# First projection by turns: keys and values over pairs of feature chunks, with the loads in that order on two queues

## The chip, the cores and the metric

One core of one Trainium2 chip runs the kernel, 1 core in all. The metric is the device time of one execution in microseconds (us). The kernel before has 923.12 us, the median of 3 runs (920.76 to 924.27).

## The reference, cut to what matters

The reference is a long chain of layers on 256 tokens of width 1024. The change touches the beginning of the first layer:

```python
h = rms_norm(x, norm_pre)                  # x: 256 tokens x 1024 features, float32
proj = h @ w_in                            # 1024 x 6936
(q_n, k_c, v_c, k_s, v_s, k_w, v_w, g_n, z_n,
 q_r, k_r, v_r, z_r, m_a, m_b) = jnp.split(proj, split_points(), axis=-1)
k_c, k_s, k_w, q_n = (rotated by position)
o_a = nsa(q_n, k_c, v_c, k_s, v_s, k_w, v_w, g_n)      # attention
o_b = retention(q_r, k_r, v_r)
x = x + rms_norm(merged @ w_out, norm_post)
```

A second layer (state space, latent attention, cross attention) and a mixture of 32 experts follow.

## The kernel before, in words

**Precision.** A product of two float32 matrices is made from three passes of a faster type: each operand is split into a high half (a rounded copy) and a low half (the rest), and `mm3` (L235 to L240) adds high by high (L238), high by low (L239) and low by high (L240). For a weight, `piece` (L219) issues the load on SP's queue (L226), ScalarE copies the high half (L231), and VectorE subtracts it to get the low half (L232). A feature chunk of x is 128 features by 256 tokens. `turn(c)` (L618) makes its two halves, on ScalarE (L619) and on VectorE (L620), and multiplies by the gain of the norm on the way.

**The first projection.** The 1024 features are eight chunks of 128. A weight piece covers a pair of chunks and one group of output columns. So a group takes four pieces. The first group, called K here, has 512 columns (three key parts and one value part, array `w1`, pieces 0 to 3). The second, V, has 280 columns (two value parts and the gates, array `w1b`, pieces 0 to 3). The third, Q, is `w1` pieces 4 to 7. K0 to K3, V0 to V3 and Q0 to Q3 are these pieces below. `tokmaj` (L242) is a generator that does one piece per step: 12 matmuls for 2 blocks of tokens, 2 chunks and 3 passes; the last step also evacuates the two PSUM banks of the group.

**Normalization.** The sum of squares per token comes from `x0`, the copy of x that is laid out by token. ScalarE squares and adds it in `scales()` (L499), GpSimd takes the power (L507), and VectorE scales the tables of cosines (L510). The results are scaled on evacuation, so the matmuls don't wait for it. `row()` (L512) turns the factors into a row with two small products on TensorE (L520).

**Order.** `early()` (L594) gives the order K0 to K3, V0 to V3, Q0 to Q3, then the rest. In the starting stage the instructions are pinned to the order of the code; afterwards a scheduler orders each engine. `self.first` holds pieces that were loaded ahead. The script of attention (L1010) weaves its steps with steps of the projection: a number means so many pieces. `keys` transposes the rotated keys (L338), `build`, `h0` to `h3` (L843) and `gelu` compress them, `queries` and `rows` are the attention itself.

**Queues.** SP's queue carries the weights and the big constants, ScalarE's queue (ACTq) the first loads of x by feature (`xT`, three loads: chunks 0 to 1, 2 to 3, 4 to 7) and the gain (`gpre`). Eight semaphores serve all loads in turn, so that the ninth load is not issued before the first has landed. The weights lie in a pool of five buffers (`w4`); a load into a used buffer waits for the low half that was made from it. Seven matmuls on a constant (`warm`, L1978) occupy TensorE until the first operands are there.

```python
w0 = self.sb("w4", [P, 2, 512])
for k in range(2):
    pin(nc.sync.dma_start(out=w0[:, k], in_=t["w1"][0][:, 512 * k:512 * k + 512]))
for c in (slice(0, 2), slice(2, 4), slice(4, 8)):
    pin(nc.scalar.dma_start(out=xT[:, c].rearrange("p k n -> p (k n)"), in_=t["xT"][:, 256 * c.start:256 * c.stop]))
```

The end of the program is the mixture of experts, whose weights (1 MB a load) come through 24 buffers.

Of the kernel before, what the change touches and what calls it, by code (L numbers as in the profile page):

```python
# [21 lines left out]
P = 128  # L22
# [79 lines left out]
def cols(v):  # L102

    return v.reshape(-1, P).T


def prepare(inp):

    a = {}
    f = {k: np.asarray(v) for k, v in inp.items()}  # L110
    g = {k[:-2]: (v[0] if v.shape[0] == 1 else v) for k, v in f.items() if k.endswith("_2")}
    a["x"] = f["x"].reshape(2, P, 1024).transpose(1, 0, 2).reshape(P, 2048)
    a["xT"] = f["x"].reshape(256, 8, P).transpose(2, 1, 0).reshape(P, 2048)
    a["gpre"] = cols(f["norm_pre"])
    a["mem"] = g["mem"].reshape(2, P, 1024).transpose(1, 0, 2).reshape(P, 2048)
    a["pos"] = g["positions"].reshape(2, P).T

# [43 lines left out]
    c = constants()  # L161
# [22 lines left out]
class K:  # L184
# [31 lines left out]
        v = self.tiles[which][:, o:o + math.prod(shape[1:])]  # L216
        return v.rearrange("p (a b) -> p a b", b=shape[-1]) if len(shape) == 3 else v.rearrange("p (a b c) -> p a b c", b=shape[-2], c=shape[-1])

    def piece(self, name, i, kc, n):  # L219

        if (name, i) in self.first:
            return self.first.pop((name, i))
        nc = self.nc
        pin = self.tc.keep_in_program_order if self.starting else lambda ins: ins
        s = self.sb("w4", [P, kc, n])
        nc.sync.dma_start(out=s.rearrange("p k n -> p (k n)"), in_=self.t[name][i])  # L226
        h = self.sb("hl", [P, 2, kc, n], F32R)
# [14 lines left out]
    def tokmaj(self, name, i0, np_, kc, n, x, evac, tag="pa"):  # L242

        ps = [self.ps(tag, [P, 512])[:, :n] for _ in range(2)]
# [225 lines left out]
    def block1(self):  # L470
        nc = self.nc
        pin, t = self.tc.keep_in_program_order, self.t


        gain = self.sb("st", [P, 8])
        xT = self.sb("a8", [P, 8, 256])


        w0 = self.sb("w4", [P, 2, 512])
        for k in range(2):  # L480
            pin(nc.sync.dma_start(out=w0[:, k], in_=t["w1"][0][:, 512 * k:512 * k + 512]))
        for c in (slice(0, 2), slice(2, 4), slice(4, 8)):
            pin(nc.scalar.dma_start(out=xT[:, c].rearrange("p k n -> p (k n)"), in_=t["xT"][:, 256 * c.start:256 * c.stop]))
            if c.start == 0:
                pin(nc.scalar.dma_start(out=gain, in_=t["gpre"]))
# [13 lines left out]
        def scales():  # L499

            ss = self.sb("sm", [P, 2])
            junk = self.sb("a8", [P, 2, 1024])
            for t in range(2):
                self.sumsq(self.x0[:, t], ss[:, t:t + 1], junk[:, t])
# [87 lines left out]
            return ev  # L592

        def early():  # L594
            yield from self.tokmaj("w1", 0, 4, 2, 512, h, ev_k)
            yield from self.tokmaj("w1b", 0, 4, 2, 280, h, ev_v)
            yield from self.tokmaj("w1", 4, 4, 2, 512, h, ev_q)
            yield from self.featmaj("w1", 8, 4, 2, h, ev_zn)
            for i in range(2):
                yield from self.tokmaj("w1", 12 + 4 * i, 4, 2, 512, h, ev_r(i))  # L600
            for nt in range(2):
                yield from self.tokmaj("w1", 20 + 4 * nt, 4, 2, 512, h, ev_vr(nt))
# [8 lines left out]
                yield from self.tokmaj("w1", 28 + 4 * nt, 4, 2, 512, h, ev_zr(nt))  # L611

        main = chain(early(), late())
        self.warm(7, idle)
        hl = self.sb("hl", [P, 2, 2, 512], F32R)
        self.first["w1", 0] = self.chunks(hl)(0), self.chunks(hl)(1)

        def turn(c):  # L618
            pin(nc.scalar.activation(hh[:, 0, c], xT[:, c], AF.Copy, scale=gain[:, c:c + 1]))  # L619
            pin(nc.vector.scalar_tensor_tensor(hh[:, 1, c], xT[:, c], gain[:, c:c + 1], hh[:, 0, c].bitcast(F32), OP.mult, OP.subtract))  # L620

        for k in range(2):
            pin(nc.scalar.activation(hl[:, 0, k], w0[:, k], AF.Copy))
            pin(nc.vector.tensor_tensor(hl[:, 1, k], w0[:, k], hl[:, 0, k].bitcast(F32), OP.subtract))
            turn(k)
        next(main)
        for i in range(1, 4):
            self.first["w1", i] = self.piece("w1", i, 2, 512)
            if i == 2:
                for j in range(2):  # L630
                    pin(nc.sync.dma_start(out=self.x0[:, j], in_=t["x"][:, j * 1024:(j + 1) * 1024]))
            turn(2 * i)
            turn(2 * i + 1)
            if i == 3:
                pin(nc.sync.dma_start(out=self.tiles["cst"], in_=t["cst"]))
                pin(nc.sync.dma_start(out=self.tiles["row"], in_=t["row"][0].partition_broadcast(P)))
                pin(nc.sync.dma_start(out=self.tiles["vec"], in_=t["vec"]))
                pin(nc.sync.dma_start(out=self.ident, in_=t["ident"]))
                scales()
            next(main)  # L640
        row()
        self.starting = False
        script, oT = self.nsa(kcv, qn, vsw, gate)
# [251 lines left out]
    def nsa(self, kcv, qn, vsw, gate):  # L895
# [73 lines left out]
        def rows(hh, g, t):  # L969
            def f():  # L970
                if t == 0:
                    s["pt", hh, g] = self.sb("a4", [P, 2, 384])
                qT, ksw, pt = s["qT"], s["ksw"], s["pt", hh, g]
                h = 4 * g + hh
                n = (t + 1) * P
                ps = self.ps("pb", [P, 2, n])
                for i in range(2):
                    nc.tensor.matmul(ps, qT[g][:, hh, t * P:(t + 1) * P], ksw[i][:, g, :, 0:n], start=(i == 0), stop=(i == 1))
                p = self.softmax(ps, 2, n, scale, cm[:, 256 - n:256], gate[:, t, 3 * h + 1:3 * h + 3])
                s["p", hh, g, t] = p  # L980
            return f
# [25 lines left out]

        flow = [(hh, g, t) for hh in range(4) for g in range(2) for t in range(2)]
        build, h0, h1, h2, h3, gelu, project = self.compress(s)
        script = [3, keys, 1, build, 2, h0, 1, h1, 1, h2, 1, h3, 1, gelu, 1, queries, rows(*flow[0]), 1, project]  # L1010
        for i, (hh, g, t) in enumerate(flow):
            if i > 0:
                script += [rows(hh, g, t), 1]
# [1126 lines left out]
```

## Time and profile before

| | |
|---|---|
| median of 3 runs | 923.12 us (920.76 to 924.27) |
| the profiled execution: its own time | 920.25 us |
| its span in the profile | 918.5 us |
| TensorE busy | 888.0 us (97%) |
| VectorE busy | 567.1 us (62%) |
| ScalarE busy | 456.9 us (50%) |
| moved by DMA | 232.17 MB, mean 253 GB/s |
| mean granted TensorE clock | 0.994 |

The profile shows one execution. Its own time is 1.75 us longer than its span, and lies 2.87 us below the median of the runs. A matmul's record ends when its last result is out, so that records overlap; how fast TensorE goes is seen from the distance between starts.

### The profile page before, as it was taken

Reading aid. Unit: us, or ns where it says so; the run is one execution under the profiler, and the core shown is the slowest. Engines: PE = TensorE matmul, PEld = TensorE weight load, DVE = VectorE, ACT = ScalarE, POOL = GpSimd, SP = SyncE. Lnnn points to the kernel's source line nnn. Section 1 sums busy time; section 2 is a strip of 40 time slices with the busy share of each in tenths; the row PEclk is TensorE's granted clock in tenths of the full one; section 3 lists DMA queues with packets and bytes.
Section 4 is the critical chain, followed back from the end, with each engine's and each line's share of the span. In section 5 each row is a group of like instructions: output and inputs, shape, how many; then the busy total and the mean of one; then the engine's idle time right before and its main releaser. Section 6 shows DMA issues by size and latency. Waiting matters only on the chain.

```text
span 918.5 us, 14740 instructions
## 1 busy us (share of the span) xinstructions
PE 888.0 (97%) x5633; PEld 697.7 (76%) x5633; DVE 567.1 (62%) x1222; ACT 456.9 (50%) x837; POOL 23.8 (3%) x43
## 2 busy tenths in 40 slices
PE   9999999999999999999999999999999999996885
PEld 6788888878899999988999897888998644442422
DVE  5689865676675999977799868556454521110103
ACT  6655666454465778777758565336453211111012
POOL 0000000100010000000000000000000000000001
PEclk9999999999999999999999999999999999999998
DMA  8945454555656554545556555668978999999994
GB/s 307 388 139 184 161 173 159 185 176 175 234 190 201 183 175 128 172 162 177 176 199 235 175 188 192 221 237 296 401 285 333 378 420 421 420 419 421 420 421 188
DMA packets 50553, 232.17 MB, mean 253 GB/s; under 512 B 6000, under 2 KB 6192, under 8 KB 37808
## 3 DMA queue, kind: packets, MB, share of 16 engines
q1 hardware_dynamic: 49760, 230.15, 68.2%
q8 instruction: 45, 0.74, 0.3%
q10 hardware_dynamic: 720, 1.05, 0.3%
q14 instruction: 28, 0.23, 0.1%
HBM read 226.95 MB, written 4.23 MB: 252 GB/s over the span
## 4 chain that ended last, share of the span: by engine, by line
PE 79%; DMA 18%; DVE 1%; ACT 1%; issue 0%; SPq 0%; POOL 0%; DVEq 0%; ACTq 0%
PE pa L238 19%; PE pa L239 19%; PE pa L240 19%; DMA wc<-in_wgu_dram 6%; DMA wf<-in_wdn_dram 4%; DMA wa<-in_wgu_dram 4%; DMA wf<-in_wdl_dram 2%; PE pb L239 2%; PE pb L240 2%; PE pb L238 2%; PE pb L1420 1%; PE pb L338 1%; PE pb L1321 1%; PE pb L2061 1%; PE pb L2024 1%; DMA w<-in_w_dram 1%
## 5 line engine op out<-in xcount | busy, mean ns | idle before, releaser
L232 DVE TENSOR_TENSOR hl<-w,hl 128x1024 fp32r<-128x1024 f32 (+3 forms) x214 | 252.1, 1186 | 112.7 <-ACT hl L231 112.2
L231 ACT ACTIVATE hl<-w 128x1024 fp32r<-128x1024 f32 (+3 forms) x214 | 218.4, 1030 | 178.3 <-PE pa L240 127.9
L238 PE MATMUL pa<-hl,a 128*128 128x512 f32 (+3 forms) x398 | 155.8, 393 | 0.3 <-ACT a L619 0.2
L239 PE MATMUL pa<-hl,a 128*128 128x512 f32 (+3 forms) x398 | 152.5, 384 | 0.4 <-DVE hl L232 0.4
L240 PE MATMUL pa<-hl,a 128*128 128x512 f32 (+3 forms) x398 | 152.3, 384 | 0.0
L238 PE MATMUL pa<-a,hl 128*128 128x256 f32 x456 | 133.3, 292 | 0.0
L239 PE MATMUL pa<-a,hl 128*128 128x256 f32 x456 | 128.7, 282 | 0.0
L240 PE MATMUL pa<-a,hl 128*128 128x256 f32 x456 | 128.6, 282 | 0.0
L238 PEld LDWEIGHTS pa<-a,hl 128*128 128x128 f32 x456 | 86.9, 191 | 1.7 <-issue 0.9
L239 PEld LDWEIGHTS pa<-a,hl 128*128 128x128 f32 x456 | 87.0, 191 | 0.4
L240 PEld LDWEIGHTS pa<-a,hl 128*128 128x128 f32 x456 | 86.9, 191 | 0.0
L238 PEld LDWEIGHTS pa<-hl,a 128*128 128x128 f32 x398 | 74.6, 188 | 15.6 <-ACT a L619 1.3
L240 PEld LDWEIGHTS pa<-hl,a 128*128 128x128 f32 x398 | 74.7, 188 | 15.1 <-DVE a L620 0.4
L239 PEld LDWEIGHTS pa<-hl,a 128*128 128x128 f32 x398 | 74.8, 188 | 14.9 <-DVE hl L232 1.7
L2067 ACT ACTIVATE vec<-pb,sm 128x256 f32<-128x256 f32 x8 | 3.8, 475 | 96.9 <-PE pb L2061 89.9
L238 PE MATMUL pa<-hl,b 128*128 128x512 f32 x128 | 51.3, 400 | 0.0
L239 PE MATMUL pa<-hl,b 128*128 128x512 f32 x128 | 50.1, 391 | 0.0
L240 PE MATMUL pa<-hl,b 128*128 128x512 f32 x128 | 50.1, 391 | 0.0
L2047 DVE TENSOR_SCALAR sm<-pb 128x1 f32<-128x1 f32 x8 | 1.3, 158 | 61.2 <-PE pb L2043 61.2
L2068 DVE SCALAR_TENSOR_TENSOR vec<-vec,pb 128x256 f32<-128x256 f32 x8 | 3.4, 421 | 53.1 <-ACT vec L2067 53.1
L397 ACT ACTIVATE a<-a,st 128x128 f32<-128x128 f32 (+1 forms) x64 | 28.5, 446 | 13.5 <-DVE st L394 13.3
L2098 PE MATMUL pa<-wz 128*128 128x512 f32 (+1 forms) x64 | 31.7, 619 | 0.1
(418 smaller groups left out, 1410.8 us busy)
## 6 DMA issues: line engine op xcount, KB each, us to landing
w<-in_w_dram SPq DMA_DIRECT2D x107, 512.0 KB, 4.1
wa<-in_wgu_dram SPq DMA_DIRECT2D x28, 1024.0 KB, 18.4
w<-in_wxkv_dram SPq DMA_DIRECT2D x16, 512.0 KB, 4.4
w<-in_wso_dram SPq DMA_DIRECT2D x16, 512.0 KB, 4.2
wa<-in_wdn_dram SPq DMA_DIRECT2D x8, 1024.0 KB, 17.5
wb<-in_wdn_dram SPq DMA_DIRECT2D x8, 1024.0 KB, 18.6
wc<-in_wgu_dram SPq DMA_DIRECT2D x8, 1024.0 KB, 19.2
wd<-in_wgu_dram SPq DMA_DIRECT2D x8, 1024.0 KB, 19.8
```

Of the source, the lines that this page charges most:

```text
L231: pin(nc.scalar.activation(hi, src, AF.Copy))
L232: pin(nc.vector.tensor_tensor(lo, src, hi.bitcast(F32), OP.subtract))
L238: mm(ps, l[0], r[0], start=first, stop=False)
L239: mm(ps, l[0], r[1], start=False, stop=False)
L240: mm(ps, l[1], r[0], start=False, stop=last)
L338: self.nc.tensor.transpose(ps[:, b, t * P:(t + 1) * P], src[t][:, c * P:(c + 1) * P], self.ident)
L397: nc.scalar.activation(p[:, i], s[:, i], AF.Exp, bias=st[:, 0, i:i + 1], scale=-1.0, accum_out=st[:, 1, i:i + 1])
L1321: nc.tensor.matmul(ps[:, b], s["q", hf][:, hh, t * P:(t + 1) * P], s["k", hf][:, hh, 0:n], start=True, stop=True)
L1420: nc.tensor.matmul(po[64 * q:64 * q + 64, b, sl], x[:, hh * 64:hh * 64 + 64], m[:, hh], start=(i < 2), stop=(i != 1))
L2024: pin(nc.tensor.matmul(g[c][:, b], self.x0[:, t, (c + b) * P:(c + b + 1) * P], s["s32"][:, t], start=(t == 0 and b == 0), stop=(t == 1 and ...
L2061: self.pinned(self.nc.tensor.matmul(s["pg"][32 * e:32 * e + 32], s["xg"][:, k, 32 * e:32 * e + 32], s["up"][k][:, e], start=(k == 0), stop ...
L2098: self.pinned(self.nc.tensor.matmul(acc[t][h][:, o:o + n], s["sT"][:, t * P:(t + 1) * P], y, start=(q == 0), stop=(q == 7)))
```

## The change

K and V go by turns: K0, V0, K1, V1, K2, V2, V3, K3. Each has its own two PSUM banks, taken ahead. The loads are issued in the order of use, on two queues: ScalarE's carries chunks 0 to 1 of x with the gain in front of them, V0, chunks 2 to 3, V1; SP's carries K0, K1, chunks 4 to 5, K2, V2, then x by token, chunks 6 to 7, V3, the constants, K3. The separate load of the gain is gone. x by feature lies in another pool (`b16`). Two pieces of Q come before `row()`, `keys` is the first step of the script, and two pieces fewer stand in the script before `h0`. There are 6 warming matmuls in place of 7.

```diff
-    a["xT"] = f["x"].reshape(256, 8, P).transpose(2, 1, 0).reshape(P, 2048)
-    a["gpre"] = cols(f["norm_pre"])
+    a["xT"] = np.concatenate([cols(f["norm_pre"]), f["x"].reshape(256, 8, P).transpose(2, 1, 0).reshape(P, 2048)], axis=1)
...
+        room = self.sb("b16", [P, 2056])
+        gain, xT = room[:, 0:8], room[:, 8:].rearrange("p (k n) -> p k n", k=8)
+        def features(c, queue=nc.scalar):
+            a = 0 if c == 0 else 8 + 256 * c
+            pin(queue.dma_start(out=room[:, a:8 + 256 * c + 512], in_=t["xT"][:, a:8 + 256 * c + 512]))
...
+        features(0)
+        pin(nc.scalar.dma_start(out=wv[0].rearrange("p k n -> p (k n)"), in_=t["w1b"][0]))
+        features(2)
+        pin(nc.scalar.dma_start(out=wv[1].rearrange("p k n -> p (k n)"), in_=t["w1b"][1]))
...
         def early():
-            yield from self.tokmaj("w1", 0, 4, 2, 512, h, ev_k)
-            yield from self.tokmaj("w1b", 0, 4, 2, 280, h, ev_v)
...
-        self.warm(7, idle)
+        self.warm(6, idle)
...
-        next(main)
-        for i in range(1, 4):
-            self.first["w1", i] = self.piece("w1", i, 2, 512)
-            if i == 2:
+        banks = [[self.ps("pa", [P, 512]) for _ in range(2)] for _ in range(2)]
+        keys = self.tokmaj("w1", 0, 4, 2, 512, h, ev_k, ps=banks[1])
+        values = self.tokmaj("w1b", 0, 4, 2, 280, h, ev_v, ps=banks[0])
+        next(keys)
+        for i in range(1, 8):
+            if i in (1, 3):
+                self.first["w1b", i // 2] = self.piece("w1b", i // 2, 2, 280, wv[i // 2])
+            elif i == 2:
+                self.first["w1", 1] = self.piece("w1", 1, 2, 512)
+                turn(2)
+                turn(3)
+                features(4, nc.sync)
+            elif i == 4:
+                self.first["w1", 2] = self.piece("w1", 2, 2, 512)
+                turn(4)
+                turn(5)
+            elif i == 5:
+                self.first["w1b", 2] = self.piece("w1b", 2, 2, 280)
                 for j in range(2):
                     pin(nc.sync.dma_start(out=self.x0[:, j], in_=t["x"][:, j * 1024:(j + 1) * 1024]))
+            elif i == 6:
+                features(6, nc.sync)
+                self.first["w1b", 3] = self.piece("w1b", 3, 2, 280)
+                turn(6)
+                turn(7)
                 pin(nc.sync.dma_start(out=self.tiles["cst"], in_=t["cst"]))
+                self.first["w1", 3] = self.piece("w1", 3, 2, 512)
...
+                scales()
+            next(keys if i in (2, 4, 7) else values)
+            if i == 6:
+                self.first["w1", 4] = self.piece("w1", 4, 2, 512)
...
+        next(main)
+        next(main)
         row()
...
-        script = [3, keys, 1, build, 2, h0, 1, h1, 1, h2, 1, h3, 1, gelu, 1, queries, rows(*flow[0]), 1, project]
+        script = [keys, 1, build, 1, h0, 1, h1, 1, h2, 1, h3, 1, gelu, 1, queries, rows(*flow[0]), 1, project]
```

SP's queue at its start, before (`w` are weights, `x` is x by token):

```order
L481 DMA w_3_105<-in_w_dram 128x512 x2
L226 DMA w_21_158<-in_w_dram 128x1024
L226 DMA w_23_179<-in_w_dram 128x1024
L631 DMA x_58<-in_x_dram 128x1024 x2
L226 DMA w_25_202<-in_w_dram 128x1024
L635 DMA cst<-in_cst_dram 128x1208
L636 DMA row<-in_row_dram 128x124
L637 DMA vec<-in_vec_dram 128x773
L638 DMA ident<-in_ident_dram 128x128
L226 DMA w_40_272<-in_w1b_dram 128x560
```

SP's queue at its start with the change (`b_1_103` holds x by feature):

```order
L486 DMA w_2_104<-in_w_dram 128x512 x2
L227 DMA w_24_174<-in_w_dram 128x1024
L482 DMA b_1_103<-in_xT_dram 128x512
L227 DMA w_27_211<-in_w_dram 128x1024
L227 DMA w_29_232<-in_w1b_dram 128x560
L648 DMA x_58<-in_x_dram 128x1024 x2
L482 DMA b_1_103<-in_xT_dram 128x512
L227 DMA w_31_252<-in_w1b_dram 128x560
L654 DMA cst<-in_cst_dram 128x1208
L227 DMA w_33_262<-in_w_dram 128x1024
```

K3 (`w_25_202` before, `w_33_262` now) moves from behind x by token to behind the constants.

ScalarE after K0, before (L231 is the high half of a weight, L619 of a chunk, L331 the sum of squares, L528 an evacuation of K):

```order
L231 ACTIVATE hl_160<-w_21_158 128x1024
L619 ACTIVATE a_5_115<-a_2_104,st_103 128x256 x2
L231 ACTIVATE hl_181<-w_23_179 128x1024
L619 ACTIVATE a_5_115<-a_2_104,st_103 128x256 x2
L331 ACTIVATE a_28_216,sm_215<-x_58 128x1024
L231 ACTIVATE hl_204<-w_25_202 128x1024
L619 ACTIVATE a_5_115<-a_2_104,st_103 128x256 x2
L331 ACTIVATE a_28_216,sm_215<-x_58 128x1024
```

ScalarE after K0 with the change:

```order
L232 ACTIVATE hl_159<-w_3_105 128x560
L232 ACTIVATE hl_176<-w_24_174 128x1024
L621 ACTIVATE a_6_116<-b_1_103 128x256 x2
L232 ACTIVATE hl_196<-w_4_106 128x560
L232 ACTIVATE hl_213<-w_27_211 128x1024
L621 ACTIVATE a_6_116<-b_1_103 128x256 x2
L232 ACTIVATE hl_234<-w_29_232 128x560
L332 ACTIVATE a_36_269,sm_268<-x_58 128x1024
L332 ACTIVATE a_37_271,sm_268<-x_58 128x1024
```

The V pieces (128x560) stand between the K pieces, and both sums of squares come together, ahead of V3, chunks 6 to 7 and K3.

## Rows read from the trace of the kernel before

**Rows 1.** The chain that ended last: start us, us, what.

```profile
6.47 8.01 DMA w<-in_w_dram
15.60 1.24 DVE hl L232
26.36 0.44 PE pb L338 x4
...
746.29 17.12 DMA wc<-in_wgu_dram
883.57 18.62 DMA wf<-in_wdl_dram
```

**Rows 2.** Waits of SP's queue, 540 us to the end: us in total, times, longest.

```profile
SPq L1841 <- PE pb L2061: 16.3, 13, 6.9
```

**Rows 3.** TensorE by time, first 45 us: start us, us, line, count, [idle before].

```profile
1.19 5.56 PE L1984 MATMUL pb<-a 128*128 128x256 f32 x14 [1.19 <-DVE it L1876]
6.94 0.73 PE L238 MATMUL pa<-hl,a 128*128 128x512 f32 x2 [0.19 <-ACT a L619]
...
20.22 0.68 PE L520 MATMUL pb<-a,cst 128*128 128x128 f32 x4 [0.40 <-PE pa L240]
...
22.22 0.29 PE L240 MATMUL pa<-hl,a 128*128 128x280 f32 x1
...
26.07 0.29 PE L240 MATMUL pa<-hl,a 128*128 128x280 f32 x1
...
28.18 0.39 PE L238 MATMUL pa<-hl,a 128*128 128x512 f32 x1
...
30.02 0.39 PE L240 MATMUL pa<-hl,a 128*128 128x512 f32 x1
...
32.97 0.39 PE L238 MATMUL pa<-hl,a 128*128 128x512 f32 x1
...
33.74 1.60 PE L843 MATMUL pb<-a,a 128*32 128x256 f32 x16
...
38.43 1.07 PE L843 MATMUL pb<-a,a 128*32 128x256 f32 x16
```

**Rows 4.** Waits of SP's queue, first 100 us.

```profile
SPq L631 <- DMA a<-in_xT_dram: 3.0, 1, 3.0
```

**Rows 5.** Stretches: us, busy of PE, PEld, DVE, ACT, POOL; clock, DMA share, GB/s.

```profile
5.00:15.00 10.00, 9.81 (x39) 7.11 (x39) 6.30 (x10) 7.42 (x13) 0.00 (x0) 1.00 1.03 410
60.00:70.00 10.00, 10.00 (x52) 8.52 (x52) 9.30 (x40) 6.04 (x16) 0.31 (x1) 1.00 0.01 2
```

**Rows 6.** ScalarE by time, with a load's issue on its queue and one on SP's.

```profile
1.67 0.46 ACTq L483 DMA_DIRECT2D a<-in_xT_dram  x1
1.67 0.42 SPq L226 DMA_DIRECT2D w<-in_w_dram  x1
...
9.20 0.91 ACT L619 ACTIVATE a<-a,st 128x256 fp32r<-128x256 f32 x2
...
12.38 1.04 ACT L331 ACTIVATE a<-x 128x1024 f32<-128x1024 f32 x1
...
19.17 1.22 ACT L231 ACTIVATE hl<-w 128x560 fp32r<-128x560 f32 x2
...
23.31 1.06 ACT L231 ACTIVATE hl<-w 128x1024 fp32r<-128x1024 f32 x1 [0.87 <-PE pa L240]
```

**Rows 7.** VectorE by time.

```profile
9.11 1.23 DVE L232 TENSOR_TENSOR hl<-w,hl 128x1024 fp32r<-128x1024 f32 x1 [0.58 <-ACT hl L231]
...
12.86 0.87 DVE L620 SCALAR_TENSOR_TENSOR a<-a,st,a 128x256 fp32r<-128x256 f32 x2
...
18.58 1.28 DVE L510 TENSOR_SCALAR cst<-cst,st 128x8 f32<-128x8 f32 x8 [0.89 <-POOL st L507]
```

**Rows 8.** Two loads issued at 1.67 us: KB, us to landing.

```profile
w<-in_w_dram SPq DMA_DIRECT2D x1, 512.0 KB, 6.3
...
a<-in_xT_dram ACTq DMA_DIRECT2D x1, 256.0 KB, 7.5
```

More of the change, by code (lines that the diff above doesn't have):

```diff
@@ L217, in spare, with piece @@
         return v.rearrange("p (a b) -> p a b", b=shape[-1]) if len(shape) == 3 else v.rearrange("p (a b c) -> p a b c", b=shape[-2], c=shape[-1])
-    def piece(self, name, i, kc, n):
+    def piece(self, name, i, kc, n, s=None):
         if (name, i) in self.first:
@@ L224, in piece @@
         pin = self.tc.keep_in_program_order if self.starting else lambda ins: ins
-        s = self.sb("w4", [P, kc, n])
-        nc.sync.dma_start(out=s.rearrange("p k n -> p (k n)"), in_=self.t[name][i])
+        if s is None:
+            s = self.sb("w4", [P, kc, n])
+            nc.sync.dma_start(out=s.rearrange("p k n -> p (k n)"), in_=self.t[name][i])
         h = self.sb("hl", [P, 2, kc, n], F32R)
@@ L240, in mm3, with tokmaj @@
         mm(ps, l[1], r[0], start=False, stop=last)
-    def tokmaj(self, name, i0, np_, kc, n, x, evac, tag="pa"):
-        ps = [self.ps(tag, [P, 512])[:, :n] for _ in range(2)]
+    def tokmaj(self, name, i0, np_, kc, n, x, evac, tag="pa", ps=None):
+        ps = [p[:, :n] for p in ps or [self.ps(tag, [P, 512]) for _ in range(2)]]
         for i in range(np_):
@@ L472, in block1 @@
         pin, t = self.tc.keep_in_program_order, self.t
-        gain = self.sb("st", [P, 8])
-        xT = self.sb("a8", [P, 8, 256])
-        w0 = self.sb("w4", [P, 2, 512])
+        room = self.sb("b16", [P, 2056])
[3 more added lines that the diff above has]
+            pin(queue.dma_start(out=room[:, a:8 + 256 * c + 512], in_=t["xT"][:, a:8 + 256 * c + 512]))
+        w0, wv = self.sb("w4", [P, 2, 512]), [self.sb("w4", [P, 2, 280]) for _ in range(2)]
         for k in range(2):
             pin(nc.sync.dma_start(out=w0[:, k], in_=t["w1"][0][:, 512 * k:512 * k + 512]))
[L482 to L485, printed above, removed]
+        features(0)
+        pin(nc.scalar.dma_start(out=wv[0].rearrange("p k n -> p (k n)"), in_=t["w1b"][0]))
+        features(2)
+        pin(nc.scalar.dma_start(out=wv[1].rearrange("p k n -> p (k n)"), in_=t["w1b"][1]))
         pin(nc.scalar.activation(self.mhalf[:, 4:8], self.mhalf[:, 0:4], AF.Tanh))
@@ L501, in scales @@
             ss = self.sb("sm", [P, 2])
-            junk = self.sb("a8", [P, 2, 1024])
             for t in range(2):
-                self.sumsq(self.x0[:, t], ss[:, t:t + 1], junk[:, t])
+                self.sumsq(self.x0[:, t], ss[:, t:t + 1], self.sb("a8", [P, 1024]))
             r = rs["col"] = self.sb("st", [P, 2])
@@ L625, in block1 @@
             turn(k)
-        next(main)
-        for i in range(1, 4):
-            self.first["w1", i] = self.piece("w1", i, 2, 512)
-            if i == 2:
+        banks = [[self.ps("pa", [P, 512]) for _ in range(2)] for _ in range(2)]
[16 more added lines that the diff above has]
+                self.first["w1b", 2] = self.piece("w1b", 2, 2, 280)
                 for j in range(2):
                     pin(nc.sync.dma_start(out=self.x0[:, j], in_=t["x"][:, j * 1024:(j + 1) * 1024]))
-            turn(2 * i)
-            turn(2 * i + 1)
-            if i == 3:
+            elif i == 6:
[3 more added lines that the diff above has]
+                turn(7)
                 pin(nc.sync.dma_start(out=self.tiles["cst"], in_=t["cst"]))
+                self.first["w1", 3] = self.piece("w1", 3, 2, 512)
                 pin(nc.sync.dma_start(out=self.tiles["row"], in_=t["row"][0].partition_broadcast(P)))
+                scales()
+            next(keys if i in (2, 4, 7) else values)
+            if i == 6:
+                self.first["w1", 4] = self.piece("w1", 4, 2, 512)
+                pin(nc.sync.dma_start(out=self.ident, in_=t["ident"]))
+                self.first["w1", 5] = self.piece("w1", 5, 2, 512)
                 pin(nc.sync.dma_start(out=self.tiles["vec"], in_=t["vec"]))
-                pin(nc.sync.dma_start(out=self.ident, in_=t["ident"]))
-                scales()
-            next(main)
+        next(main)
+        next(main)
         row()
```

## The prediction

> **What bounds the kernel now.** I read the views in this order. The chain of waits first, for what sets the end. Its last part is loads of expert weights back to back, from 746.29 us to the one that lands at 902.2 (883.57 + 18.62) [rows 1]. That does not make the beginning worthless: until then SP's queue waits for TensorE to release buffers (16.3 us in 13 waits for L2061 alone) [rows 2]. The stream begins when TensorE has come so far, and its end moves with that. So a microsecond won at the beginning is won at the end, as long as TensorE stays the bound in between.
>
> TensorE by time comes next. In a steady stretch a matmul of 512 columns starts every 0.227 us (13 starts from 30.02 to 32.97), one of 280 columns every 0.128 us (30 starts from 22.22 to 26.07) [rows 3]. K is 48 of the first kind, 10.9 us, V 48 of the second, 6.1 us, together 17.0. But from the first one at 6.94 to the first of Q at 28.18 pass 21.24 us [rows 3]. Between them stand also two small products of `row` and eight transposes, some 12 narrow records at 0.44 us for four [rows 1], 1.3 us. The rest, 21.24 - 17.0 - 1.3 = 2.9 us, is waiting. What it waits for, the chain says: the load issued at 6.47 us that lands at 14.48 is K3, and the low half that ends at 16.84 follows from it (L232) [rows 1]. K3 was issued late, since SP's queue stood 3.0 us for a semaphore that a load of x had [rows 4]. A second wait is at 20.22, where TensorE idles 0.40 us ahead of `row` [rows 3].
>
> **The change part by part.**
>
> *The start.* TensorE's first matmul waited for L619 (0.19 us idle in the record) [rows 3]; L619 had waited for the separate load of the gain. The gain now comes in front of the first chunks. I take the first matmul at 6.6 us instead of 6.94. One warming matmul less takes off 5.56 / 7 = 0.79 us at most [rows 3], ending the warming at 6.0; it lies in the shadow of the first operands and costs nothing. If that cover is gone, because TensorE's clock needed it, the first 12 matmuls would start at twice 0.227 us, at 1.2 in place of 2.4 GHz, and 2.7 us are lost; the clock column reads 1.00 in the stretch from 5 us [rows 5].
>
> *The loads.* They run at 410 GB/s in all [rows 5], which is 400 KB per us. Up to and with K3 the change loads 5824 KB in place of 4100 KB (before, K0 to K2, x by feature, the gain and x by token stood ahead of K3; now V and the constants do too, and the gain rides with x). 1724 KB more are 4.3 us, so K3 lands at 14.5 + 4.3 = 18.8 us. It is needed only after K0 to V3, that is after 6.6 + 36 x 0.227 + 48 x 0.128 = 20.9 us.
>
> How the two queues share decides when the early pieces land. K1 (512 KB on SP's queue) and a load of 256 KB on ScalarE's were issued in the same moment, 1.67 us [rows 6]; the large one landed at 8.0, the small one at 9.2 [rows 8]. So they don't share by bytes, else the small one had been first; rather whole loads take turns. I take turns, and 400 KB per us from 5.6 us on: second half of K0 6.2, V0 6.9, K1 8.2, chunks 2 to 3 8.9, chunks 4 to 5 9.5, V1 10.2, K2 11.5, V2 12.2, x by token 14.8, chunks 6 to 7 15.4, V3 16.1, constants 17.6. With equal bytes K1 would be there at 9.5 and TensorE would lose 0.4 us more in K1.
>
> The Trainium skill, "DMA: Bandwidth & Descriptors", section "Queues, rings and completion order", says that each DMA engine goes round the queues packet by packet; the two landings agree with that, and by it the end of K3 would be the 24.1 us below rather than 24.5. The same page of the Trainium skill, "Issuing engines are not separate DMA queues", speaks against a second queue: it saves issue time alone, no bandwidth. Nothing above counts on bandwidth from it.
>
> *ScalarE and VectorE.* Per K piece ScalarE needs 1.06 + 0.91 us (weight, two chunks), per V piece 0.61 (1.22 / 2), and 1.04 us for each sum of squares [rows 6]; VectorE needs 1.23 + 0.87 for a K piece, some 0.7 for a V piece (scaled from 1.23 by columns), and 1.28 for the tables [rows 7]. In the new order ScalarE handles x by token (landed 14.8) until 16.3, V3 until 17.0, chunks 6 to 7 until 17.9, K3 from 18.9 to 19.9. VectorE first waits for GpSimd's power (0.89 us before) [rows 7] until some 17.5, then V3 18.2, chunks 19.0, tables 20.3, K3 21.5. TensorE reaches V3 at 19.4 and K3 at 20.9. It does the one matmul that needs no low half and waits until 21.5. K3 ends at 21.5 + 11 x 0.227 = 24.0; with 0.1 for the waits in K0, 24.1 us.
>
> *The narrow work.* `row` and the eight transposes still cost 1.3 us, now amid Q, where there are no such waits; I leave 0.3 us for starting them. Equal work is then done at 24.1 + 1.3 + 0.3 = 25.7 us instead of 28.18: -2.5 us.
>
> *After that.* Q0 and Q1 are loaded behind K3, some 1.3 us each and the constants between them, landing by 20.4 and 22; TensorE needs them at 24.1 and 27. No cover is lost. `h0` took 1.60 us before and the same work 1.07 later [rows 3], since the load behind it was late; two more pieces stand ahead of it now, so I take 0.3 of these 0.5 us. Sum: -2.8 us. Attention as a whole stands two pieces (5.5 us) later in TensorE's order and starts 2.5 us earlier by the clock, so its own steps come some 3 us later; the two pieces are missing at the end of the layer, where TensorE has other work in line. At nothing, then, as long as TensorE is the bound there.
>
> **Bounds.** Most: no waiting from 6.6 on, 23.6 for K3, nothing for starting narrow work (23.6 + 1.3 against 28.18), 0.5 at `h0`: -3.8 us. Least: 0, if all of it is waited for elsewhere. I take -2.8, near the upper end, because each load but K3 lands well before its use. The profiled execution would go from 920.25 to 917.45. It lies 2.87 us below the median of the runs, 923.12; against that median I forecast **920.3 us**.
>
> **The rivals.**
>
> *The gain is eaten in attention.* From 60 to 70 us VectorE is busy 9.30 of 10 us [rows 5], close to a bound of its own. If the steps of attention, now later, set the pace there, the 2.8 us are lost again: 923 us. Against it: TensorE is busy 10.00 of 10 there too, with projection pieces between the steps, and has no less work.
>
> *K3 arrives too late, and the kernel is slower.* Its load waits on SP's queue for the buffer of V1 (its low half, some 11.8 us by my times), with everything behind it. A load took 8.01 us from issue to landing [rows 1]. From 11.8 that is 19.8, which costs 1 us. Each microsecond beyond 19 is one on TensorE's path; the gain is used up at about 21.8. If the SP queue stalls twice, at V2's buffer and at this one, for 3.0 us each as before [rows 4], K3 lands at 24 to 25 and ends past 29, later than before by 1 us or more after its narrow work: 924.5 us. For it: V2, V3 and K3 now each wait for a low half on VectorE. Against it: at 12 us there are still 5 us of loads in line.
>
> *It gains more.* The waits of TensorE in attention also shrink because two pieces lie ready more: 2 us more, 918.
>
> *It doesn't do what it says:* the order of the engines shows that the turns are there, so I give this nothing.
>
> **How the numbers follow.** Forecast 0.62; eaten 0.18; slower by late loads 0.10; more 0.10. About 0.5% (4.6 us) is what a measurement of this kernel can tell from no change; the three runs shown lie 3.5 us apart. Faster by over 0.5% means below 918.5: half of "more", a fifth of the forecast by scatter of the medians, 0.17 in all. Slower by over 0.5% means above 927.7: a part of the late loads, 0.06. Within: 0.77. The range reaches down to the largest gain with some scatter, 917.2, and up to the case of late loads, 924.2.
>
> **What would show it.** Right: the chain of waits has no load of K3 in it; the first matmul at 6.6; K and V together take 17 to 18 us with starts at 0.227 and 0.128 us; Q's first matmul at about 24; the stream of expert weights begins some 3 us earlier and goes at the same rate. Wrong: idle TensorE ahead of V3 or K3 (the load, or VectorE behind the tables); first starts at 0.45 us apart (the clock); an equal end of K3 but an unchanged start of the expert stream (attention).

## The result

The change has 926.34 us (median of 13 runs, 924.21 to 928.27); before, in the same comparison, 921.77 us (13 runs). The ratio is 1.0054, 95% interval 1.0043 to 1.0065: slower by 4.6 us, where 920.3 us was forecast. The profiled execution took 926.27 us with a span of 924.5 us (before 918.5).

The start went as forecast or better. TensorE by time (start us, us, engine, line, operation, shape, count, [idle before]):

```profile
5.61 0.73 PE L239 MATMUL pa<-hl,a 128*128 128x512 f32 x2
...
8.51 0.29 PE L239 MATMUL pa<-hl,a 128*128 128x280 f32 x1
...
10.78 0.50 PE L240 MATMUL pa<-hl,a 128*128 128x512 f32 x1 [0.35 <-DVE hl L233]
...
23.86 0.62 PE L239 MATMUL pa<-hl,a 128*128 128x512 f32 x2
```

Against [rows 3] the first matmul is 1.3 us earlier and Q's first 4.3 us (two pieces of Q now precede `row` and the transposes, some 1.3 us of narrow work). The only wait of the engine is the 0.35 us at K1. The load of K3 landed at 18.75 us, and ScalarE took it at once:

```profile
18.86 1.06 ACT L232 ACTIVATE hl<-w 128x1024 fp32r<-128x1024 f32 x1 [1.33 <-DMA w<-in_w_dram]
```

In the chain of waits no load of K3 stands any more, only K1's; the last expert load begins 5.4 us later than in [rows 1]:

```profile
1.67 6.71 DMA w<-in_w_dram
...
888.98 19.19 DMA wf<-in_wdl_dram
```

So the time is lost between. A count over the whole trace shows where: for each matmul the distance to the next start, less the steady distance of its shape (0.227 us for 512 columns, and so on: the lower quartile of the distances behind that shape in the kernel before), added up by stretch. Before loses 12.2 us of TensorE up to 50 us, the change 9.3: 2.9 won. From 50 to 110 us before loses 5.0, the change 9.5; from 170 to 210 us before 2.0, the change 6.9. Elsewhere the two agree within 0.5 us. The stretches (us, busy of PE, PEld, DVE, ACT, POOL, clock, DMA share, GB/s), first before, then the change:

```profile
70.00:80.00 10.00, 10.00 (x51) 8.41 (x50) 9.37 (x26) 5.11 (x11) 0.00 (x0) 1.00 0.90 297
...
190.00:200.00 10.00, 10.00 (x49) 7.96 (x48) 6.76 (x9) 5.23 (x7) 0.00 (x0) 1.00 0.64 193
```

```profile
70.00:80.00 10.00, 7.94 (x27) 5.75 (x26) 9.82 (x25) 1.63 (x3) 0.00 (x0) 0.83 0.43 135
...
190.00:200.00 10.00, 7.57 (x30) 5.90 (x29) 7.17 (x10) 3.33 (x5) 0.56 (x1) 0.83 0.52 156
```

In these two stretches TensorE now idles 2.1 and 2.4 us, and its granted clock falls. **The first loss**, TensorE of the change:

```profile
72.26 0.61 PE L239 MATMUL pa<-hl,a 128*128 128x512 f32 x2
73.57 0.73 PE L239 MATMUL pa<-hl,a 128*128 128x512 f32 x2 [0.69 <-ACT hl L232]
75.67 0.50 PE L240 MATMUL pa<-hl,a 128*128 128x512 f32 x1 [1.37 <-DVE hl L233]
...
76.51 0.63 PE L241 MATMUL pa<-hl,a 128*128 128x512 f32 x1
76.94 0.63 PE L239 MATMUL pa<-hl,a 128*128 128x512 f32 x1
```

It waits for a high and a low half, and then starts matmuls 0.43 us apart, until 79.9 us: 1.2 in place of 2.4 GHz. The low half decides: the high half is there by 73.57 us, the low half only at 75.62. VectorE in that time:

```profile
67.32 1.22 DVE L233 TENSOR_TENSOR hl<-w,hl 128x1024 fp32r<-128x1024 f32 x1
...
68.84 0.40 DVE L381 TENSOR_TENSOR a<-pa,cst 128x256 f32<-128x256 f32 x1
...
73.54 0.42 DVE L386 TENSOR_TENSOR a<-a,a 128x256 f32<-128x256 f32 x1
...
74.41 1.21 DVE L233 TENSOR_TENSOR hl<-w,hl 128x1024 fp32r<-128x1024 f32 x1
```

Between two low halves stand 5.9 us of other work: 12 operations of the rotation (L381 to L386, called ropes below) of retention's first operands, amid a softmax. **The second loss**:

```profile
178.30 1.46 PE L820 MATMUL pb<-a,a 128*128 128x256 f32 x6
...
180.46 0.59 PE L822 MATMUL pb<-a,a 128*128 128x256 f32 x2
...
195.54 0.84 PE L339 MATMUL pb<-ident,a 128*128 128x128 f32 x4 [2.43 <-DVE a L595]
196.03 0.78 PE L241 MATMUL pa<-hl,a 128*128 128x512 f32 x1
196.61 0.63 PE L239 MATMUL pa<-hl,a 128*128 128x512 f32 x1
```

Three steps of retention (the last ones, `outs`, L820 and L822) stand together at 178 to 181 us, each with normalizations on VectorE behind it. These push back what follows there:

```profile
187.87 0.99 DVE L831 TENSOR_SCALAR a<-pb,sm,sm 128x256 f32<-128x256 f32 x2 [0.87 <-POOL sm L327]
...
192.88 1.22 DVE L233 TENSOR_TENSOR hl<-w,hl 128x1024 fp32r<-128x1024 f32 x1
194.02 0.68 DVE L593 SCALAR_TENSOR_TENSOR a<-a,pa 128x512 f32<-128x512 f32 x1
194.74 0.75 DVE L595 SCALAR_TENSOR_TENSOR a<-a,st,a 128x512 f32<-128x512 f32 x1
```

TensorE takes its work in order: the transposes (L339) wait for L595, and the next piece stands behind them.

### The profile page after: what moved, and what is told of

Same layout as the page of the kernel before. It is cut to its first block, busy times and chain, and to the rows that moved or that the text cites. A ratio compares the mean times of both kernels' runs of the same rounds, so it can differ in the third digit from the quotient of the medians.

```text
span 924.5 us, 14745 instructions
## 1 busy us (share of the span) xinstructions
PE 890.0 (96%) x5631; PEld 700.1 (76%) x5631; DVE 567.7 (61%) x1222; ACT 456.0 (49%) x837; POOL 23.8 (3%) x43
## 4 chain that ended last, share of the span: by engine, by line
PE 82%; DMA 11%; DVE 3%; issue 1%; ACT 1%; POOL 0%; SPq 0%; DVEq 0%; ACTq 0%; POOLq 0%
PE pa L239 19%; PE pa L241 19%; PE pa L240 19%; DMA wc<-in_wgu_dram 4%; PE pb L2086 3%; DMA wa<-in_wgu_dram 2%; DMA wf<-in_wdn_dram 2%; DMA wf<-in_wdl_dram 2%; PE pa L2123 2%; PE pb L2049 2%; PE pb L2111 2%; PE pb L240 2%; PE pb L241 2%; PE pb L239 2%; PE pb L1445 1%; PE pb L339 1%
## 5 line engine op out<-in xcount | busy, mean ns | idle before, releaser
L232 ACT ACTIVATE hl<-w 128x1024 fp32r<-128x1024 f32 (+3 forms) x214 | 218.7, 1030 | 183.2 <-PE pa L241 132.8
L239 PE MATMUL pa<-hl,a 128*128 128x512 f32 (+3 forms) x398 | 156.4, 395 | 0.7 <-ACT hl L232 0.7
L239 PE MATMUL pa<-a,hl 128*128 128x256 f32 x456 | 133.4, 293 | 0.0
L239 PEld LDWEIGHTS pa<-a,hl 128*128 128x128 f32 x456 | 86.9, 191 | 2.6 <-issue 1.8
L240 PEld LDWEIGHTS pa<-hl,a 128*128 128x128 f32 x398 | 75.7, 190 | 16.5 <-DVE hl L233 2.7
L239 PEld LDWEIGHTS pa<-hl,a 128*128 128x128 f32 x398 | 75.6, 190 | 15.2 <-ACT hl L232 1.1
L241 PEld LDWEIGHTS pa<-hl,a 128*128 128x128 f32 x398 | 75.5, 190 | 15.2 <-DVE a L622 0.4
L239 PE MATMUL pa<-hl,b 128*128 128x512 f32 x128 | 51.2, 400 | 0.0
L2049 PEld LDWEIGHTS pb<-wz,x 128*128 128x128 f32 x224 | 28.0, 203 | 5.9 <-PE pb L2086 3.4
```

The source lines that it names most:

```text
L239: mm(ps, l[0], r[0], start=first, stop=False)
L2049: pin(nc.tensor.matmul(g[c][:, b], self.x0[:, t, (c + b) * P:(c + b + 1) * P], s["s32"][:, t], start=(t == 0 and b == 0), stop=(t == 1 and ...
```

## The experiments

Theory 1 was at first: the script alone costs it, by the place of attention and by the pieces left for retention. Eighteen kernels ran; each ratio is to before, run beside it (medians 920.4 to 921.3), with its 95% interval. The pieces of the projection that stand between steps of attention or retention are called fillers. The table at the end of this section has TensorE's loss by stretch for all.

**1. Four kernels with the places put back, alone and together.** In the first, attention stands where it stood:

```diff
-        next(main)
-        next(main)
+        next(main)
         row()
-        script = [keys, 1, build, 1, h0, 1, h1, 1, h2, 1, h3, 1, gelu, 1, queries, rows(*flow[0]), 1, project]
+        script = [keys, 1, build, h0, 1, h1, 1, h2, 1, h3, 1, gelu, 1, queries, rows(*flow[0]), 1, project]
```

> Turns and loads as in the change, but h0 comes after two pieces of Q again, as before (one piece ahead of row, none between build and h0). Theory 1: the start is 2.8 us faster, and the loss is made by the script alone, which puts attention two pieces later and leaves seven pieces in place of nine among the steps of retention; then both losses of TensorE (4.2 us from 70 us on, 4.2 us from 190 us on) go: 921.8 - 2.8 = 919.0 us, ratio to before 0.997, under 1 us lost in each of the two stretches. Theory 2: the turns and the loads disturb what follows (buffers, order of the queues): 926 us, ratio 1.005, both losses stay. Theory 3: the two losses have nothing to do with the pieces but are accidents of the scheduler's order: one or both move elsewhere, 921 to 926 us.

Measured: 921.05 us, ratio 0.9996 (0.9985 to 1.0008). Both losses are gone, but the start's gain too: 2.4 us ahead at 20 us, level at 50. TensorE there:

```profile
31.38 0.73 PE L239 MATMUL pa<-hl,a 128*128 128x512 f32 x2
33.04 0.50 PE L240 MATMUL pa<-hl,a 128*128 128x512 f32 x1 [0.93 <-DVE hl L233]
...
34.36 1.43 PE L867 MATMUL pb<-a,a 128*32 128x256 f32 x16
```

The loads of h0 (1 MB) went ahead of this piece's weight; they land back to back, 1.28 us for each 512 KB, at 392 to 411 GB/s from 15 to 40 us. The weight landed at 28.96 us, 3.2 us later than in the change. But ScalarE, at work for `build`, took it only at 30.27 us, and VectorE began the low half at 31.78. Loads and the two engines both hold it up; which of them decides was not tested.

The second leaves attention late and takes two pieces out of its end:

```diff
-            if i in (3, 5, 7, 9, 11, 13,):
+            if i in (3, 5, 7, 9):
```

> The change, with two pieces fewer amid the last rows of attention (steps 11 and 13), so that nine stand among the steps of retention again; attention begins two pieces later as in the change. Theory 1: the loss from 190 us on goes, that from 70 us on stays: 926.3 - 4.2 = 922.1 us, ratio to before 1.000. Theory 2: 926 us, both stay. Theory 3: 922 to 926 us, and the loss at 190 us does not follow the number of pieces.

Measured: 923.11 us, 1.0022 (1.0007 to 1.0037). The second loss is gone, the first is there with the same two waits (0.69 and 1.37 us), 2.6 us.

The third is the kernel before with the shift:

```diff
-        script = [3, keys, 1, build, 2, h0, 1, h1, 1, h2, 1, h3, 1, gelu, 1, queries, rows(*flow[0]), 1, project]
+        script = [3, keys, 1, build, 4, h0, 1, h1, 1, h2, 1, h3, 1, gelu, 1, queries, rows(*flow[0]), 1, project]
```

> The kernel before, its start untouched, with two more pieces ahead of h0 in the script: attention two pieces later, seven pieces among the steps of retention. Theory 1: both losses come: 921.8 + 8.4 = 930.2 us, ratio to before 1.009, 4 us lost from 73 to 83 us and 4 us from 193 to 203 us. Theory 2: 921.8 us, ratio 1.000, no loss. Theory 3: between 921 and 930.

Measured: 924.57 us, 1.0044 (1.0028 to 1.0059). The second loss comes (the transposes wait 2.45 us for the same line), the first doesn't. VectorE's order has 21 low halves ahead of the first rope there, the change 20 (before 24). So the shift alone doesn't make the first loss. Whether the earlier start makes it, or the one low half less ahead of the ropes, this pair doesn't separate; part 4 bears on it. Theory 1 (both losses, 930.2 us) missed.

The fourth is the first one with two pieces put into attention's end (`if i in (3, 5, 7, 9, 11, 12, 13, 14)`):

> As the first of these runs (h0 after two pieces of Q as before), with two pieces more amid the last rows of attention, so that seven stand among the steps of retention. Theory 1: only the loss from 190 us on comes: 919.0 + 4.2 = 923.2 us, ratio to before 1.0015. Theory 2: 926 us. Theory 3: no loss at 190 us, or one elsewhere: 919 to 926 us.

Measured: 924.15 us, 1.0028 (1.0016 to 1.0039): the second loss alone, again a wait of 2.44 us.

**2. Can the gain be kept?** Two pieces ahead of h0 as in the change, two fewer behind h3; then the same in the kernel before:

```diff
-        script = [keys, 1, build, 1, h0, 1, h1, 1, h2, 1, h3, 1, gelu, 1, queries, rows(*flow[0]), 1, project]
+        script = [keys, 1, build, 1, h0, 1, h1, 1, h2, 1, h3, gelu, queries, rows(*flow[0]), 1, project]
```

> The change, with the two pieces that it puts ahead of h0 taken out again behind h3 (none between h3, gelu and queries); so the loads of h0 to h3 have the same cover of pieces as in the change, attention proper and retention stand against the pieces as before. Theory 1, revised: the run with all positions back lost the 2.4 us of the start between 30 and 50 us, where the loads follow each other every 1.28 us and h0 to h3 need 4 MB; there bytes set the pace, and two pieces more ahead of h0 cover them. Then this kernel keeps the gain (2.5 to 2.9 us less lost by TensorE up to 50 us than before), and has neither of the losses at 70 and 190 us: 921.0 - 2.7 = 918.3 us, ratio to before 0.997. Rival (attention on VectorE eats the gain whatever the script is): the 2.7 us are lost between 50 and 110 us: 921.0 us, ratio 1.000.

Measured: 923.85 us, 1.0031 (1.0016 to 1.0045). The gain is there at 50 us (9.6 against 12.2) and lost by 110: TensorE waits 3.03 us for one low half at 65 to 68.5 us. No ropes stand there (the first begins at 79 us); VectorE is at work for attention's softmax. The rival was right in kind, but the loss is larger than it said: 4.3 us more than before from 50 to 110 us, not 2.7.

> The kernel before, its start untouched, with the same shift and return in its script: two pieces more ahead of h0, two fewer behind h3. Theory 1, revised: the shift alone covers some of the waits of h0 to h3 (the earlier run of before with the shift lost 0.8 us less up to 50 us) and brings no loss at 70 and 190 us: 920.2 us, ratio 0.999; the turns are worth the rest. If the turns are worth nothing and the script all: 918.3 us, as with the turns.

Measured: 921.93 us, 1.0013 (1.0001 to 1.0025): 0.9 us won up to 50 us, lost later; 920.2 was expected.

**3. The second loss at its cause.**

```diff
-        self.weave(self.spread(self.retention(qk, s), 10), main)
+        self.weave(self.spread(self.retention(qk, s), 7), main)
```

> The change, with retention's ten steps woven with seven pieces over all ten steps, where the change asks for ten, runs out after seven and does the last three steps without any. Theory 1: the loss at 190 us comes from these last three steps (outs) standing together, which piles their work up on VectorE; with a piece behind each of the last three, nothing is lost there: 926.0 - 4.2 = 921.8 us, ratio to before 1.001. Rival (seven pieces are too few wherever they stand): 926 us, ratio 1.0054.

Measured: 923.83 us, 1.0022 (1.0010 to 1.0033). With seven pieces still, nothing is lost from 190 us on. The `outs` stand apart, and the transposes don't wait:

```profile
171.92 1.02 PE L820 MATMUL pb<-a,a 128*128 128x256 f32 x4
175.55 0.59 PE L820 MATMUL pb<-a,a 128*128 128x256 f32 x2
...
192.15 0.66 PE L339 MATMUL pb<-ident,a 128*128 128x128 f32 x4
```

It is the clump, not the number.

**4. The first loss: VectorE.** In the first kernel of this part `ev_r(0)` copies on ScalarE in place of the rotation, so that its results differ from the reference's (fillers as in the second run):

```diff
+                if i == 0:
+                    nc.scalar.activation(qk[i][:, t], ps, AF.Copy)
+                    return
```

> As the run with the fillers late only (nine pieces in retention, attention two pieces later), and the rotation of the first group of retention's operands is left out: 12 operations of VectorE of 0.33 us, one copy by ScalarE for each block in their place. Theory 1: the loss from 70 us on is VectorE, which does these 12 ahead of a low half that TensorE waits for; without them TensorE loses under 1 us from 70 to 80 us, and the run is some 2 to 3 us faster than the 923.1 with them: 920 to 921 us. Rival (ScalarE's late high half or the weight's load is what TensorE waits for): 2.6 us or more are still lost from 70 to 80 us, 923 us.

Measured: 919.96 us, 0.9984 (0.9972 to 0.9997). The first loss is gone (0.4 us from 70 to 80 us) and the gain of the start lives on.

Then the rotation as a whole, but on GpSimd: the first group, both groups, both in the kernel before, and both in the change with the seven pieces spread evenly.

```diff
+                    y = self.sb("a2", [P, 512])
+                    nc.scalar.activation(y, ps, AF.Copy)
+                    self.rope(out, y.rearrange("p (h d) -> p h d", h=4), heads, half, cos, sin, nc.gpsimd)
```

> As the run with the fillers late only (923.1 us), and the 12 operations of the first group's rotation run on GpSimd, from a copy that ScalarE makes; nothing is left out. Theory 1: as with the rotation left out, the loss from 70 us on goes and the gain of the start is kept: 920.0 us, ratio to before 0.999. Rival (GpSimd beside VectorE slows VectorE's operations, so that its time there stays as long): 923 us, with VectorE's operations between 70 and 80 us longer than before (a low half over 1.23 us).

> As the run before this one, with both groups' rotations (24 operations) on GpSimd. Theory 1 (VectorE sets the pace of attention between 60 and 110 us): TensorE loses 1 us less than with the first group alone between 80 and 110 us, 919.0 us, ratio to before 0.998. Rival: no further gain, 920 us, or a loss where the order of the scheduler changes, 922 us.

> The kernel before with both groups' rotations on GpSimd; its start and its script untouched. Theory 1 (the gain of the turns is kept where VectorE has room, and the turns are worth 2.5 us): this one has VectorE's relief without the earlier start: 921.0 us, 0 to 1 us better than before, and 1.5 to 2 us behind the same with the turns. Rival (the relief of VectorE is the gain and the turns are worth nothing): as fast as with the turns, 919 us.

> The change as it stands, with the seven pieces of retention spread evenly and both rotations on GpSimd: each of the two losses is taken away at its own cause, and the script stays. Theory 1: 926.0 - 4.2 - 2.6 = 919.2 us, ratio to before 0.998. Rival: retention with seven pieces stays slower by 1 us, 920 us; or the scheduler's order makes a new loss, 922 us.

Measured: 926.34 us, 1.0057 (1.0043 to 1.0070); 926.89 us, 1.0064 (1.0047 to 1.0081); 925.70 us, 1.0053 (1.0035 to 1.0071); 926.31 us, 1.0060 (1.0045 to 1.0075). All four are slower, and by more than the rivals said (at most 923 us). VectorE's operations grow longer beside GpSimd, as the first of these rivals had it: in the first of the four,

```profile
70.84 2.83 DVE L404 TENSOR_SCALAR a<-a,st 128x256 f32<-128x256 f32 x4
...
79.40 1.74 DVE L233 TENSOR_TENSOR hl<-w,hl 128x1024 fp32r<-128x1024 f32 x1
```

and the same lines without GpSimd, in the second run:

```profile
69.52 1.00 DVE L404 TENSOR_SCALAR a<-a,st 128x256 f32<-128x256 f32 x4
...
74.29 1.22 DVE L233 TENSOR_TENSOR hl<-w,hl 128x1024 fp32r<-128x1024 f32 x1
```

These four could not tell whether VectorE's load eats the gain. So the multiplications by the softmax denominator (32 of 0.25 to 0.3 us) went to ScalarE instead: half of them, all (both with fillers as in the second run), all with two pieces taken out later, all in the kernel before.

```diff
-            nc.vector.tensor_scalar(p[:, i], p[:, i], st[:, 2, i:i + 1], None, OP.mult)
+            nc.scalar.activation(p[:, i], p[:, i], AF.Copy, scale=st[:, 2, i:i + 1])
```

> As the run with the fillers late only (923.1 us), and ScalarE, not VectorE, does half of the 32 multiplications by the softmax denominator (0.25 to 0.3 us each on VectorE). Theory 1 (VectorE sets the pace of attention, and relief that doesn't come from GpSimd gives the 2.5 us of the start back): 4 us of VectorE's work less over 60 to 130 us; up to 1 us of the loss at 70 us stays, since only two of the moved operations lie ahead of it: 921.5 us, ratio to before 1.000. Rival (what costs there is the one pile-up of the 12 rope operations, not VectorE's load as such): 923 us.

> As the run before this one with all 32 on ScalarE. Theory 1: 920.5 us, ratio to before 0.999, the loss from 70 to 80 us under 1.5 us. Rival (ScalarE, on which the high halves stand, becomes the next late one): 923 us or more, TensorE waits for high halves.

> As the run with the two pieces taken out later (923.9 us), and all 32 multiplications on ScalarE. Theory 1: of the 4.3 us lost from 60 to 70 us 2 to 3 go: 921 us, ratio to before 1.000. Rival: TensorE waits for the same low half as long, 924 us.

> The kernel before with all 32 multiplications on ScalarE, nothing else changed. Theory 1: before has no losses at 60 to 80 us to take away; 0 to 1 us better, 920.5 us, ratio 0.9995. Rival (the relief by itself is worth as much as with the turns): 918.5 us.

Measured: 921.30 us, 1.0006 (0.9991 to 1.0021); 920.73 us, 0.9996 (0.9982 to 1.0011); 922.49 us, 1.0012 (0.9998 to 1.0026); 921.04 us, 0.9999 (0.9986 to 1.0011). The loss from 50 to 110 us goes down with the load that is taken off: 8.0, 6.6, 6.0 us with none, half and all; at the wait itself, from 70 to 80 us, 2.6, 1.8 and 1.2 us. There with none and with all:

```profile
70.00:80.00 10.00, 7.93 (x34) 5.91 (x33) 10.00 (x26) 2.44 (x3) 0.00 (x0) 1.00 0.40 132
```

```profile
70.00:80.00 10.00, 9.30 (x41) 7.15 (x40) 9.93 (x24) 4.07 (x7) 0.00 (x0) 1.00 0.49 154
```

Up to 170 us it is 15.8, 15.0 and 14.4 us, so part of what goes before 110 us comes back behind it. The kernel before gains nothing by the same relief. So at the wait it is VectorE's load. In the third of the four only 1.0 us of 9.3 went, where 2 to 3 of the 4.3 from 60 to 70 us were expected; why, no run shows.

Last, the order of the projection's groups (fillers as in the second run): a gate and retention's values, which ScalarE evacuates, ahead of the two rotated groups. The second rotated group then comes behind `trig`, which has overwritten the cosine tables by that time, so its values differ; kind, number and size of the operations are the same.

```diff
         def early():
...
+            for nt in range(2):
+                yield from self.tokmaj("w1", 36 + 4 * nt, 4, 2, 512, h, ev_gate("ta", nt))
             for nt in range(2):
                 yield from self.tokmaj("w1", 20 + 4 * nt, 4, 2, 512, h, ev_vr(nt))
         def late():
+            for i in range(2):
+                yield from self.tokmaj("w1", 12 + 4 * i, 4, 2, 512, h, ev_r(i))
```

> As the run with the fillers late only (923.1 us), with the groups of the projection in another order: the first gate's four and retention's values, which ScalarE evacuates alone, come ahead of retention's two rotated groups, whose 24 operations of VectorE so fall behind the stretch from 60 to 110 us in which VectorE is 8 to 10 of 10 us busy. Nothing is left out. Theory 1 (VectorE's load in attention eats the gain of the start): as in the run without the first rotation, under 1 us is lost from 70 to 80 us, TensorE's loss up to 110 us is 2 us or more below that of before, and the run takes 919.5 us, ratio to before 0.9985. Rival (the scheduler's order puts another wait there, or retention now waits for its rotated operands near 170 us): 922 us or more.

> The kernel before with the same order of the groups, its start and script untouched. Theory 1: without the turns there is no earlier start to keep; 921 us, ratio to before 1.000, 1.5 to 2 us behind the same order with the turns. Rival (the order alone is the gain): as fast as with the turns.

Measured: 919.38 us, 0.9980 (0.9970 to 0.9990), and without the turns 921.76 us, 1.0007 (0.9995 to 1.0018). The two differ by 2.4 us. Most of that is the start: up to 50 us 9.2 us are lost with the turns and 12.6 without. But the first also has attention two pieces later, and that shift alone gave 0.8 to 0.9 us up to 50 us in the kernel before. With the turns, from 70 to 80 us:

```profile
70.00:80.00 10.00, 9.78 (x46) 7.88 (x45) 8.92 (x23) 4.69 (x7) 0.00 (x0) 1.00 0.89 281
```

VectorE is no longer full (8.92 us), and TensorE idles 0.22 us.

TensorE's lost time by stretch, us (counted as above, one profiled execution each):

| kernel | 0 to 50 | 50 to 110 | 110 to 170 | 170 to 210 | ratio |
|---|---|---|---|---|---|
| before | 12.2 | 5.0 | 7.0 | 2.0 | 1 |
| the change | 9.3 | 9.5 | 7.0 | 6.9 | 1.0054 |
| positions back | 12.4 | 5.0 | 6.9 | 1.9 | 0.9996 |
| fillers late only | 9.2 | 8.0 | 7.8 | 2.5 | 1.0022 |
| before, shifted | 11.4 | 5.6 | 7.0 | 6.9 | 1.0044 |
| retention short only | 11.9 | 5.4 | 5.3 | 6.7 | 1.0028 |
| two taken out later | 9.6 | 9.3 | 7.6 | 2.6 | 1.0031 |
| before, two taken out later | 11.3 | 6.2 | 7.5 | 2.4 | 1.0013 |
| seven spread evenly | 9.6 | 8.3 | 8.2 | 1.8 | 1.0022 |
| no first ropes | 9.3 | 5.3 | 8.3 | 1.9 | 0.9984 |
| first ropes on GpSimd | 9.3 | 12.7 | 7.2 | 2.9 | 1.0057 |
| all ropes on GpSimd | 9.2 | 13.3 | 7.2 | 2.9 | 1.0064 |
| before, ropes on GpSimd | 12.5 | 7.9 | 7.5 | 2.7 | 1.0053 |
| seven spread evenly, ropes on GpSimd | 9.3 | 13.6 | 7.1 | 2.8 | 1.0060 |
| half of scaling on ScalarE | 9.4 | 6.6 | 8.4 | 1.9 | 1.0006 |
| all scaling on ScalarE | 9.2 | 6.0 | 8.4 | 1.9 | 0.9996 |
| two taken out later, scaling on ScalarE | 9.3 | 8.3 | 7.6 | 2.6 | 1.0012 |
| before, scaling on ScalarE | 12.4 | 5.0 | 7.6 | 2.6 | 0.9999 |
| ropes later | 9.2 | 5.0 | 8.3 | 1.9 | 0.9980 |
| before, ropes later | 12.6 | 4.7 | 7.3 | 2.3 | 1.0007 |

## Why the prediction was wrong

**The start was right.** Equal work was forecast 2.5 us earlier, the sum with `h0` 2.8; TensorE lost 2.9 us less up to 50 us, and the same sixteen pieces with `h0` to `h3` are done 2.7 us earlier (other work taken off). The terms: first matmul 5.61 (forecast 6.6; the first halves of K0 and x landed at 4.50 and 4.68); K1 landed at 8.38, chunks 2 to 3 at 8.62, V1 at 10.06, K3 at 18.75 (forecast by turns 8.2, 8.9, 10.2, 18.8); Q at 23.86 (24.1). In this profile the six warming matmuls sufficed: from 7.10 us on starts are 0.23 us apart. That was partly luck. In the profile of "seven spread evenly", which has the same start, the warming ran 0.43 us apart to its last start at 6.04 us. The first product, whose operands were ready at 5.90, began at 6.11; starts were slow until 7.2, and 4.2 us were lost up to 10 us in place of 3.2. The clock column reads 1.00 in the stretch from 5 us there too, so only the starts tell it. K and V took 18.25 us, just over the 17 to 18 named.

**The step that failed** is the one behind the sum: "the two pieces are missing at the end of the layer, where TensorE has other work in line. At nothing, then, as long as TensorE is the bound there." It failed twice.

In attention TensorE was not the bound. [rows 5] had VectorE 9.30 of 10 us busy, and TensorE 10.00 because a stock of low halves was ready. In the kernel before (L232 makes the low half there, L239 uses it):

```profile
55.11 1.23 DVE L232 TENSOR_TENSOR hl<-w,hl 128x1024 fp32r<-128x1024 f32 x1 [0.24 <-ACT hl L231]
...
67.86 1.20 DVE L232 TENSOR_TENSOR hl<-w,hl 128x1024 fp32r<-128x1024 f32 x1
```

```profile
69.80 0.39 PE L239 MATMUL pa<-hl,a 128*128 128x512 f32 x1
```

From 56.34 to 67.86 us VectorE makes no low half, and TensorE lives on three that are ready. The next is ready at 69.06 us for a matmul at 69.80: 0.7 us to spare. The earlier start uses up that stock. In the change VectorE's order also has the ropes ahead of a low half (the first at 68.84 us; before, at 78.48). The piece begun at 72.26 us has its low half at 75.62, and from 50 to 110 us 4.5 us more are lost than before, where 2.9 had been won. How much of it is the earlier start and how much the place of the ropes in that order, no pair of runs separates. The loss in attention is the rival "eaten in attention", which had a chance of 0.18 and the right engine; its price, all of the gain, was 1.6 us short. In "fillers late only", where the same waits came and the clock did not fall, 3.0 us are lost, about the gain. That VectorE is the engine is shown by the runs with less on it, the runs of before with the same relief and, though the shift of two pieces is in it too, the last pair.

At the end of the layer the two pieces did cost: 4.9 us. Retention asks for ten pieces; nine were left before and one step stood without, now seven and three. I had counted that TensorE has other work, not what the clump does to VectorE, and that TensorE's in-order queue has transposes ahead of that other work. This case was not among the rivals. The balance: -2.9 + 4.5 + 4.9 = 6.5 us for the profiled executions, whose spans differ by 6.0; the medians by 4.6.

**The other rivals.** The K3 rival gave about the right time for a wrong reason: nothing waited for K3. "It gains more" did not happen.

**What stays open.** Ten of the kernels, three of them made from before, lose 0.5 to 1.4 us more from 110 to 170 us (7.5 to 8.4 against 7.0). Part of that may be a loss that has only moved past 110 us; no run was aimed at it. A kernel that beats both with its rotation intact was not found: the last order needs its tables kept elsewhere, which was not tried. Of those with the turns that compute everything, "positions back", "half of scaling on ScalarE" and "all scaling on ScalarE" are level with before.

## What to carry to other kernels

A start that is won moves every later meeting of the engines; look in the busiest later stretch at the engine that is 9 of 10 us busy behind a full TensorE before counting the gain as kept. Where fillers are handed out from a shared stock, count how many are left at its end and which steps then stand together. Relief for VectorE was worth nothing here where nothing was early, and the earlier start nothing where VectorE was full. Both together gave 0.2% in two kernels whose results differ from the reference's (no first ropes, ropes later); with the scaling on ScalarE, where all is computed, they only came level.

## What the runs showed of the hardware

GpSimd beside VectorE slows it: four multiplications of 128x256 took 2.83 us in place of 1.00, a low half up to 1.74 in place of 1.22, while single operations of GpSimd on 128x256 took 0.74 to 1.72 us. VectorE's operations with an operand in PSUM (L983 there, 0.21 us) and its reductions (L985, 0.28 us) did not grow longer. The Trainium skill, "SBUF — State Buffer", section "SBUF: two separate sides", says that VectorE and GpSimd share a pair of ports: a VectorE operation in a two-port mode, or one with two inputs in SBUF against a GpSimd operation that reads SBUF, and a GpSimd operation lock each other out for a whole instruction. The longer and the unchanged durations agree with that; no run here tests it further.

TensorE's clock is not the same after the same wait. Waits of 2.43 to 2.45 us at 190 us were followed by a stretch at 1.2 GHz in all three kernels that have them (mean clock 0.83 of 190 to 200 us); the waits of 0.69 and 1.37 us at 73 to 76 us were in the change (0.83), but not in "fillers late only" and "seven spread evenly" (0.69 and 1.34 us), where the stretch from 70 to 80 us reads 1.00. From 70 to 80 us the change loses 4.2 us, "fillers late only" 2.6: 1.6 us of difference between two profiles with the same waits.
